# Prompt pages inside the first pair's compression products, head norms from two float32r parts, and the gates' two weight parts side by side

## The chip, the core and the metric

The kernel runs on one core of a Trainium2 chip. The metric is the device time of one execution in microseconds (us). Five engines work side by side, each through its own queue in order: PE (matrix products; PEld loads its weights), DVE (vector), ACT (scalar), POOL (GpSimd) and SP, which here only issues transfers. PE writes its products to banks of PSUM; DVE or ACT must read a bank out ("evacuate" it) before PE may reuse it.

## The reference, cut to what matters

Two layers of a decoder, for a prompt of 256 tokens and for 8 samples of 8 new tokens each, 320 columns together. The change lies in the input projection of layer 0 alone, whose parts are:

```python
z = jnp.einsum('btd,de->bte', h, W['w_in'])
rx, rg, q, kc, vc, ks, vs, kw, vw, gl = _split_even(z)
q  = _rmsnorm(q.reshape(b_, t, N_HEADS, HEAD_DIM), W['q_norm'])      # per head of 64
ks = _rmsnorm(ks.reshape(b_, t, N_KV, HEAD_DIM), W['k_norm'][1])     # kw likewise
gates = jax.nn.sigmoid(gl.astype(F32))                               # 48 columns

def _compress(k, pe, w1, w2):   # k: blocks of 64 tokens; the samples' come from cache pages
    kb = k.reshape(b_, t // BLOCK, BLOCK, N_KV, HEAD_DIM) + pe
    hid = jax.nn.gelu(jnp.einsum('bnjgd,jde->bnge', kb, w1))
    return jnp.einsum('bnge,ef->bngf', hid, w2)
```

`_compress` is done for keys and for values, over 64 cache pages of 128 tokens (of the samples) and the prompt's two pages of 128 tokens.

## The kernel before

**Products in three.** A float32 product is made from float32r parts: weights are split into `whi` (ACT, line 145) and `wlo` (DVE, line 146), activations into `yh` and `yl`, and PE does whi by yl, wlo by yh and whi by yh (lines 204 to 206). One such product has 128 by 128 weights and 320 columns.

**Groups and slots.** The projection goes in groups of 256 output columns, in the order kc, vc, ks, kw, q0, q1, q2, q3, gates (128 columns wide, though 48 are used), vs, vw. A group takes 16 steps of 128 rows of weights, 96 products. After every 24 of them (four steps) comes a **slot**: `side()` runs what the table `at(n, function, ...)` has put there, in the order in which the table was written. A group is four slots, the gates two; `E` holds each group's first slot after its last product: ks 12, kw 16, q0 20, q1 24, q2 28, q3 32, gates 34, vs 38. The work done in slots is in the program order of each engine, so it stands in the engine's queue between two stretches of 24 products.

**Evacuation.** At a group's end DVE multiplies its two banks by `rt` into SBUF (line 817 for k and v, line 882 for q). PE has three banks for groups, two in use by each, so the second half of the next group's first products needs the first of these two evacuations.

**Compression.** Cache pages come in four pairs (`bp` 0 to 3), each for keys and values (`i` 0, 1) in two halves of 8 pages (tile `cx`). `cmp_swap` rearranges a half into `cy` with four copies (line 703), two on DVE, one on POOL, one on ACT; `cmp_mm` multiplies it by `w1` (line 713: 16 steps by 2 outputs, 32 plain float32 products of 128 columns, of which the trace shows 64 rows, two each). The halves are swapped at the slot of a group's end and the next (12 and 13, 16 and 17, ...), the product comes two slots later (15, 19, ..., and 11 for the first). `cmp_mm` then adds the two outputs at once: a copy by ACT (line 719), an addition by DVE (line 720), twice. The prompt's pages and the position rows `pe` are a fifth pair with its own copies and its own products of 24 columns (slots 13 and 15). `w1` is loaded by SP (`cmp_load_w`, slots 7 and 11).

**Head norms.** For each 128 rows of k or q (two per group, "even" and "odd" below): ACT squares them (line 826, `hsq`, both in the slot of the group's end), PE sums over heads with a plain float32 product by the block matrix `blk1` (line 831), ACT takes the root (line 833), DVE the reciprocal (line 834) and the scaling (lines 845 and 847 for k, 891 and 895 for q). For q the even product is in the slot after the group's end and the odd one in the second; for k both are in the slot after.

Of the kernel before, what the change touches and what calls it, by code (L numbers as in the profile page):

```python
# [70 lines left out]
def tile_hybrid_step(ctx: ExitStack, tc: tile.TileContext, A, O, stop=None, dbg=None):  # L71
# [31 lines left out]
    plan(w_in, 0, 16, [4528], 128, 8)  # L103
# [33 lines left out]
    def w_conv():  # L137
        u, hf = divmod(st["conv"], 2)
        if st["dma"] == u:
            w_dma()  # L140
        st["conv"] += 1
        r = (raws.popleft() if hf else raws[0])[:, hf * HW:hf * HW + HW]
        h = wp.tile([128, HW], F32R, name="whi", bufs=NSP)
        l = wp.tile([128, HW], F32R, name="wlo", bufs=NSP)
        S.copy(h, r)  # L145
        (G if u < 4 and hf == 0 else V).tensor_tensor(l, r, h.bitcast(F32), ALU.subtract)  # L146
        convs.append((h, l))
# [65 lines left out]

    def run(gen):
# [10 lines left out]
    blk1 = cm[:, C_BLK:C_BLK + 128]  # L225
    ones = cst.tile([128, 128], F32, name="ones")
# [247 lines left out]
    rec = wab = None  # L474
# [3 lines left out]
    pct = cst.tile([128, 192], F32, name="pct")  # L478
# [3 lines left out]
    def rec_open():  # L482
        nonlocal rec, wab
        rec = rgp.enter_context(pool("rec"))
        wab = rec.tile([128, 2, 8, 128], F32, name="wab")
        SP.dma_start(wab[:, 0], A["rg_wa"][0].rearrange("h i j -> i h j"))
# [179 lines left out]
    def cmp_w():  # L666
# [3 lines left out]
        w2 = cmp_.tile([128, 128], F32, name="w2")  # L670
# [16 lines left out]
    def cmp_load_p():  # L687

        for i in range(2):
            cx[4, i, 0] = x = tok["kv"[i] + "c"]  # L690
            G.memset(x[64:128, 2], 0.0)
            SP.dma_start(x[0:64, 2], A["cmp_pe_" + "kv"[i]][0].rearrange("j g d -> j (g d)"))

    def cmp_swap(bp, i, hf, pages):
        v = cx.pop((bp, i, hf))[:, :pages].rearrange("p n (g s d) -> p (n g) s d", g=4, s=2)
        if bp == 4:
            cx["y", bp, i] = yf[:, 1560 * i:1560 * i + 768].rearrange("p (d h s n) -> p d h s n", h=1, s=2, n=12)
        elif hf == 0:
            cx["y", bp, i] = cmp_.tile([128, 32, 2, 2, 32], F32, name="cy")
        y = cx["y", bp, i][:, :, hf]  # L700
# [5 lines left out]
    def cmp_mm(bp, i, pages):  # L706

        y = cx.pop(("y", bp, i)).rearrange("p d h s n -> p d (h s n)")
        p = bank("a")
        n = pages * 8  # L710
# [4 lines left out]
        nh = min(pages, 8)  # L715
        for k in range(pages // nh):
            h = hid[64 * i:64 * i + 64, 16 * bp + 8 * k:16 * bp + 8 * k + nh].rearrange("p n g s -> p s (n g)")
            q = p[:, 64 * k:64 * k + 8 * nh].rearrange("p (s n) -> p s n", s=2)
# [3 lines left out]
    def cmp_gelu():  # L722
# [10 lines left out]
        cx["sq"] = cmp_.tile([128, 264], F32, name="csq")  # L733
        cx["vr"] = cmp_.tile([128, 4, 4, 4], F32, name="vr")
# [89 lines left out]
    def head_square(key, src):  # L824
        sq = evp.tile([128, N], F32, name="hsq", bufs=2)
        S.activation(sq, src, AF.Square)
        evt["sq", key] = sq

    def head_scale(key):
        p = bank("a")  # L830
        PE.matmul(p[:, :N], blk1, evt.pop(("sq", key)), start=True, stop=True)
        rs = evp.tile([128, N], F32, name="hrs", bufs=2)
# [4 lines left out]
    def k_square(b):  # L837
        for c in range(2):
            head_square((b, c), evt["k" + b][:, c])

    def k_norm(b):
        nm_ = "k" + b
        for c in range(2):
# [848 lines left out]
```

## Time and profile before

| | |
|---|---|
| time, median of 3 executions (lowest to highest) | 2909.09 us (2905.2 to 2910.19) |
| the profiled execution: its time, and its span from first to last instruction | 2911.25 us, 2909.6 us |
| PE busy, share of the span | 2846.3 us, 98% |
| DVE, ACT, POOL busy | 1618.6, 1213.1, 378.2 us |
| mean granted TensorE clock | 0.990 of full speed |
| moved by the DMA engines | 463.98 MB |

PE is busy nearly always, so a time is read as PE's products plus the waits between them. Rows of products overlap: a product's row lasts about 0.31 us while the next one starts 0.147 us later, so counts of starts tell the pace and not the rows' length.

### The profile page before, as it was taken

The page shows a single profiled execution, that of the slowest core. Times are in us where ns is not written, and L with a number is a line of the kernel's source. Part 1 is how long each engine was busy: PE and PEld are TensorE (multiplying, and loading weights), DVE is VectorE, ACT ScalarE, POOL GpSimd, SP SyncE. Part 2 cuts the span into 40 slices and gives each one's busy share as a digit, 9 for nine tenths or more (in the row PEclk, how much of TensorE's full clock was granted, in tenths as well). Part 3 has the DMA queues.
Part 4 walks back from the last instruction along what each step waited for, and adds up shares of the span by engine and source line. Part 5 has one row for each costly group of instructions (what it writes and reads, how often), then busy time and mean ns, then how long its engine had stood idle before and what let it go on. Part 6 is the DMA issues. An engine that isn't in the chain of part 4 may idle for free.

```text
span 2909.6 us, 53661 instructions
## 1 busy us (share of the span) xinstructions
PE 2846.3 (98%) x20947; PEld 2785.6 (96%) x20947; DVE 1618.6 (56%) x2937; ACT 1213.1 (42%) x2336; POOL 378.2 (13%) x555
## 2 busy tenths in 40 slices
PE   8999987999999999999999999999999999999999
PEld 7998776899999999999999999999999999999999
DVE  6796677774444544544465555555444444544544
ACT  4555644354334434434443333344433433433433
POOL 2323353230010010010010111111011011001000
PEclk9999989999999999999999999999999999999999
DMA  8765258645445555555445444444444444544543
GB/s 244 213 198 156 73 147 257 210 138 162 165 154 167 165 159 161 165 166 153 153 144 156 152 147 150 147 153 148 149 152 145 153 152 149 149 152 148 149 157 119
DMA packets 275997, 463.98 MB, mean 159 GB/s; under 512 B 19050, under 2 KB 100694, under 8 KB 275215
## 3 DMA queue, kind: packets, MB, share of 16 engines
q1 hardware_dynamic: 268254, 438.47, 49.1%
q0 software_dynamic: 6864, 19.44, 2.1%
q8 instruction: 164, 2.69, 0.4%
q10 hardware_dynamic: 624, 2.64, 0.2%
q14 instruction: 91, 0.74, 0.1%
HBM read 452.95 MB, written 15.92 MB: 161 GB/s over the span
## 4 chain that ended last, share of the span: by engine, by line
PE 81%; DVE 0%; DMA 0%; ACT 0%; issue 0%; DVEq 0%; ACTq 0%
PE ps_g L204 27%; PE ps_g L206 27%; PE ps_g L205 27%; DMA wraw<-in_w_out_e_dram 0%; PE ps_a L1652 0%; DVE wlo L146 0%; PE ps_a L1264 0%; PE ps_o L1325 0%; PE ps_a L1307 0%; DVE ktl L1168 0%; PE ps_a L633 0%; PE ps_a L1624 0%; DVE rs L1473 0%; PE ps_a L436 0%; DVE y L1475 0%
## 5 line engine op out<-in xcount | busy, mean ns | idle before, releaser
L146 DVE TENSOR_TENSOR wlo<-wraw,whi 128x512 fp32r<-128x512 f32 x1488 | 1007.4, 718 | 1122.3 <-ACT whi L145 1121.5
L145 ACT CAST whi<-wraw 128x512 fp32r<-128x512 f32 x1492 | 854.1, 617 | 1377.8 <-PE ps_g L206 1334.0
L204 PE MATMUL ps_g<-yl,whi 128*128 128x320 f32 x3408 | 1066.9, 313 | 10.9 <-DVE kv L817 5.1
L205 PE MATMUL ps_g<-yh,wlo 128*128 128x320 f32 x3408 | 1056.8, 310 | 0.0
L206 PE MATMUL ps_g<-yh,whi 128*128 128x320 f32 x3408 | 1056.6, 310 | 0.0
L204 PE MATMUL ps_g<-xl,whi 128*128 128x320 f32 x2560 | 796.2, 311 | 11.3 <-DVE xl L446 7.3
L206 PE MATMUL ps_g<-xh,whi 128*128 128x320 f32 x2560 | 792.7, 310 | 0.0
L205 PE MATMUL ps_g<-xh,wlo 128*128 128x320 f32 x2560 | 792.7, 310 | 0.0
L204 PEld LDWEIGHTS ps_g<-yl,whi 128*128 128x128 f32 x3408 | 643.2, 189 | 22.3 <-issue 8.4
L205 PEld LDWEIGHTS ps_g<-yh,wlo 128*128 128x128 f32 x3408 | 643.3, 189 | 1.7 <-issue 0.2
L206 PEld LDWEIGHTS ps_g<-yh,whi 128*128 128x128 f32 x3408 | 643.2, 189 | 0.0
L204 PEld LDWEIGHTS ps_g<-xl,whi 128*128 128x128 f32 x2560 | 482.4, 188 | 13.1 <-DVE xl L446 7.7
L205 PEld LDWEIGHTS ps_g<-xh,wlo 128*128 128x128 f32 x2560 | 482.4, 188 | 0.0
L206 PEld LDWEIGHTS ps_g<-xh,whi 128*128 128x128 f32 x2560 | 482.1, 188 | 0.0
L1477 POOL TENSOR_TENSOR y<-y,rs 128x320 f32<-128x320 f32 x96 | 92.3, 994 | 1257.8 <-DVE rs L1473 1257.8
L1473 DVE TENSOR_TENSOR rs<-ps_g,r 128x320 f32<-128x320 f32 x128 | 60.6, 488 | 25.1 <-PE ps_g L206 25.0
L1506 DVE TENSOR_TENSOR fr<-fr 128x320 f32<-128x320 f32 x128 | 62.3, 487 | 11.1 <-ACT xh L1509 11.1
L431 POOL TENSOR_TENSOR nacc<-nacc,nsq 128x320 f32<-128x320 f32 x45 | 44.1, 980 | 172.0 <-ACT nsq L427 170.4
L1507 DVE TENSOR_TENSOR xl<-fr,xh 128x320 fp32r<-128x320 f32 x128 | 62.9, 492 | 4.4
L1509 ACT ACTIVATE xh<-fr 128x320 fp32r<-128x320 f32 x128 | 60.3, 471 | 4.1
L1503 ACT ACTIVATE fr<-ps_g 128x320 f32<-128x320 f32 x128 | 56.1, 438 | 5.7 <-PE ps_g L206 5.7
L1586 POOL TENSOR_TENSOR xx<-cg,r 128x256 f32<-128x256 f32 x16 | 13.1, 819 | 278.4 <-DVE xx L1584 278.4
(382 smaller groups left out, 1426.3 us busy)
## 6 DMA issues: line engine op xcount, KB each, us to landing
wraw<-in_w_ff_dram SPq DMA_DIRECT2D x512, 512.0 KB, 3.7
wraw<-in_w_in_o_dram SPq DMA_DIRECT2D x96, 512.0 KB, 3.7
wraw<-in_w_in_e_dram SPq DMA_DIRECT2D x74, 512.0 KB, 5.3
wraw<-in_w_out_e_dram SPq DMA_DIRECT2D x32, 512.0 KB, 5.5
wraw<-in_w_out_o_dram SPq DMA_DIRECT2D x32, 512.0 KB, 3.9
cx<-in_cache_cmp_k_dram SPq DMA_DIRECT2D x64, 128.0 KB, 2.1
cx<-in_cache_cmp_v_dram SPq DMA_DIRECT2D x64, 128.0 KB, 3.4
kl<-in_cache_sel_k_dram SPq DMA_DIRECT2D x64, 128.0 KB, 3.6
```

The costliest lines, as they stand in the source:

```text
L145: S.copy(h, r)
L146: (G if u < 4 and hf == 0 else V).tensor_tensor(l, r, h.bitcast(F32), ALU.subtract)
L204: PE.matmul(ps[m][:, :N], wh, al, start=k + j == 0, stop=False)
L205: PE.matmul(ps[m][:, :N], wl, ah, start=False, stop=False)
L206: PE.matmul(ps[m][:, :N], wh, ah, start=False, stop=k + j == nk - 1)
L431: G.tensor_tensor(nacc["t"], nacc["t"], sq, ALU.add)
L1473: V.tensor_tensor(t, ps[:, :N], scale, ALU.mult)
L1477: after(1, lambda: G.tensor_tensor(y[:, c], y[:, c], t, ALU.add))
L1503: S.activation(t, ps[:, :N], AF.Relu)
L1506: V.tensor_tensor(t, t, t, ALU.mult)
L1507: V.tensor_tensor(xl[:, c], t, xh[:, c].bitcast(F32), ALU.subtract)
L1509: after(1, lambda: S.activation(xh[:, c], t, AF.Square))
```

## The change

Four things are changed, all in the input projection:

- The prompt's pages and the `pe` rows become columns 128 to 147 of the first pair's products (`cmp_swap_p`); the fifth pair and its products are gone. `pe` is no longer loaded into the token tile but into free space of `yf`, and it, `w1` and `w2` are loaded from POOL's queue and no longer from SP's.
- The additions behind a compression product (`cmp_evac`) are moved one slot later and joined into one copy and one addition for 128 columns; the first pair has two more small ones of each, for the prompt and `pe`.
- A head's squares are split into `hsh` (ACT) and `hsl` (DVE), and PE sums them in two float32r products by `blkr`, a copy of `blk1`. Only the even squares are made at the group's end; the odd ones are made in the slot after, behind the even reciprocal. For k the odd product moves to the second slot, as it was for q.
- The gates are planned as 64 columns. `whi` and `wlo` lie side by side as one set of 128 weights, so that two products (by yl and by yh) do what three did; `gate_evac` adds the two halves of the result.

```diff
-    plan(w_in, 0, 16, [4528], 128, 8)
+    plan(w_in, 0, 16, [4592], 64, 16)
...
+        if units[u][4] == 64:
+
+            for d, q in ((h, r[:, :256]), (l, r[:, 256:])):
+                d, q = (x.rearrange("p (k f) -> p k f", k=4) for x in (d, q))
+                S.copy(d[:, :, :64], q)
+                V.tensor_tensor(d[:, :, 64:], q, d[:, :, :64].bitcast(F32), ALU.subtract)
+            return
...
+    def gemm_64(act, evac):
+
+        ps = bank("g")
+        for hf in range(2):
+            w_fill()
+            st["half"] += 1
+            for i, w in enumerate(convs.popleft()):
+                for j in range(4):
+                    k = 8 * hf + 4 * i + j
+                    for m, x in enumerate(act(k)[::-1]):
+                        PE.matmul(ps[:, :N], w[:, 128 * j:128 * j + 128], x, start=k + m == 0, stop=k + m == 16)
...
-            SP.dma_start(w1[64 * hf:64 * hf + 64, i], A["cmp_w1_" + nm_][0][:, 32 * hf:32 * hf + 32])
-        SP.dma_start(w2[64 * i:64 * i + 64, 64 * i:64 * i + 64], A["cmp_w2_" + nm_][0])
+            G.dma_start(w1[64 * hf:64 * hf + 64, i], A["cmp_w1_" + nm_][0][:, 32 * hf:32 * hf + 32])
+        G.dma_start(w2[64 * i:64 * i + 64, 64 * i:64 * i + 64], A["cmp_w2_" + nm_][0])
...
+    def cmp_swap_p(i):
+
+        v = tok["kv"[i] + "c"][:, 0:2].rearrange("p n (g s d) -> p (n g) s d", g=4, s=2)
+        e = cx["pe"][:, i].rearrange("p (g s d) -> p g s d", g=4, s=2)
+        y = cx["y", 0, i]
+        for half in range(2):
+            h_ = slice(64 * half, 64 * half + 64)
+            for s_ in range(2):
+                (S.copy if s_ == half else V.tensor_copy)(
+                    y[h_, :, 128 + 8 * s_:136 + 8 * s_], v[64 * s_:64 * s_ + 64, :, half].rearrange("p n d -> p d n"))
+            G.tensor_copy(y[h_, :, 144:148], e[:, :, half].rearrange("p g d -> p d g"))
...
+        n = 128 if bp else 148
         for d in range(16):
             for u in range(2):
-                PE.matmul(p[64 * u:64 * u + 64, :n], w1[:, i, 16 * u + d], y[:, 16 * u + d],
+                PE.matmul(p[64 * u:64 * u + 64, :n], w1[:, i, 16 * u + d], y[:, 16 * u + d, :n],
                           start=d == 0, stop=d == 15)
...
+        if (bp, i) == (3, 1):
+            cmp_evac(bp, i, p)
+        else:
+            at(st["slot"] + 1, cmp_evac, bp, i, p)
...
     def head_square(key, src):
-        sq = evp.tile([128, N], F32, name="hsq", bufs=2)
+        sq = evp.tile([128, N], F32, name="hsq")
+        h = evp.tile([128, N], F32R, name="hsh", tag="hrs", bufs=2)
+        l = evp.tile([128, N], F32R, name="hsl")
         S.activation(sq, src, AF.Square)
-        evt["sq", key] = sq
+        split(h, l, sq)
+        evt["sq", key] = (l, h)
 
     def head_scale(key):
         p = bank("a")
-        PE.matmul(p[:, :N], blk1, evt.pop(("sq", key)), start=True, stop=True)
+        for i, x in enumerate(evt.pop(("sq", key))):
+            PE.matmul(p[:, :N], blkr, x, start=i == 0, stop=i == 1)
...
     def q_square(g):
-        for c in (2 * g, 2 * g + 1):
-            head_square(("q", c), evt["q", c])
+        head_square(("q", 2 * g), evt["q", 2 * g])
 
     def q_norm(c):
         t = evt["q", c]
         rs = head_scale(("q", c))
+        if c % 2 == 0:
+            head_square(("q", c + 1), evt["q", c + 1])
...
-            at(n + 6, cmp_mm, bp, i, 16)
+            at(n + 6, cmp_mm, bp, i)
...
-    at(E["vc"] + 2, cmp_load_p)
-    for i in range(2):
-        at(E["vc"] + 4, cmp_swap, 4, i, 0, 3)
-        at(E["vc"] + (7 if i else 5), cmp_mm, 4, i, 3)
+    at(CN + 1, cmp_load_p)
     for b in "sw":
         n = E["k" + b]
-        at(n, k_square, b)
-        at(n + 1, k_norm, b)
+        for c in range(2):
+            at(n + c, k_square, b, c)
+            at(n + 1 + c, k_norm, b, c)
```

DVE's queue over group q0, from its evacuation (line 882 before, 927 after) on; before:

```order
L882 TENSOR_TENSOR qr<-ps_g,rt 128x320 x2
L703 COPY cy<-cx 64x32x32 x2
L146 TENSOR_TENSOR wlo<-wraw,whi 128x512 x2
L703 COPY cy<-cx 64x32x32 x2
L834 RECIPROCAL hrs<-hrs 128x320
L891 SCALAR_TENSOR_TENSOR qp<-qr,qg,hrs 128x2x128
L895 SCALAR_TENSOR_TENSOR qbd<-qr,qg,hrs 64x8x8 x2
L146 TENSOR_TENSOR wlo<-wraw,whi 128x512 x2
L834 RECIPROCAL hrs<-hrs 128x320
```

and of the change:

```order
L927 TENSOR_TENSOR qr<-ps_g,rt 128x320 x2
L724 COPY cy<-cx 64x32x32 x2
L471 TENSOR_TENSOR hsl<-hsq,hsh 128x320
L762 TENSOR_TENSOR yr<-ps_a,yr 64x2x2x32
L154 TENSOR_TENSOR wlo<-wraw,whi 128x512 x2
L724 COPY cy<-cx 64x32x32 x2
L880 RECIPROCAL hrs<-hrs 128x320
L471 TENSOR_TENSOR hsl<-hsq,hsh 128x320
L937 SCALAR_TENSOR_TENSOR qp<-qr,qg,hrs 128x2x128
L941 SCALAR_TENSOR_TENSOR qbd<-qr,qg,hrs 64x8x8 x2
L154 TENSOR_TENSOR wlo<-wraw,whi 128x512 x2
L880 RECIPROCAL hrs<-hrs 128x320
```

The even low part `hsl` now stands behind the first two page copies, the odd one behind both pairs of copies, two weight splits and the even reciprocal; the joined addition (line 762) has come in front of the weight splits.

PE's queue in slot 13, which is behind the group ks (`ps_g` are the projection's banks, `ps_a` those of the work in slots; lines 211 to 213 of the change are 204 to 206 of before); before:

```order
L206 MATMUL ps_g<-yh,whi 128x320
L713 MATMUL ps_a<-yr,w_571 64x24 x32
L831 MATMUL ps_a<-hsq,cm 128x320 x2
L204 MATMUL ps_g<-yl,whi 128x320
L205 MATMUL ps_g<-yh,wlo 128x320
```

and of the change:

```order
L213 MATMUL ps_g<-yh,whi 128x320
L877 MATMUL ps_a<-hsl,blkr 128x320
L877 MATMUL ps_a<-hsh,blkr 128x320
L211 MATMUL ps_g<-yl,whi 128x320
L212 MATMUL ps_g<-yh,wlo 128x320
```

The prompt's 32 products of 24 columns are gone, the even norm's one product has become two, with the low part `hsl` first, and the odd norm's pair follows 24 products of the projection later.

POOL's queue from the output of kc on (slot 6); before:

```order
L862 DMA out_dram<-tok 128x2x256
L866 DMA out_dram<-tok 64x256
L703 COPY cy<-cx 64x32x32 x2
L862 DMA out_dram<-tok 128x2x256
L866 DMA out_dram<-tok 64x256
```

and of the change:

```order
L907 DMA out_dram<-tok 128x2x256
L911 DMA out_dram<-tok 64x256
L715 DMA yr<-in_cmp_pe_k_dram 64x256
L715 DMA yr<-in_cmp_pe_v_dram 64x256
L704 DMA w_571<-in_cmp_w_k_dram 64x2048 x2
L705 DMA yr<-in_cmp_w_k_dram 64x64
L724 COPY cy<-cx 64x32x32 x2
```

The loads of `pe` and of the keys' `w1` stand between the output of kc and POOL's first page copies.

## Rows read from the trace of the kernel before

**Rows 1.** The page, busy us of PE, its share of the span, its products.
```profile
PE 2846.3 (98%) x20947; PEld 2785.6 (96%) x20947; DVE 1618.6 (56%) x2937; ACT 1213.1 (42%) x2336; POOL 378.2 (13%) x555
```

**Rows 2.** PE's waits, 0 to 300 us: waiter, releaser, us, times, longest.
```profile
PE ps_g L204 <- DVE kv L817: 5.1, 2, 4.2
PE ps_a L713 <- DMA w<-in_cmp_w_k_dram: 4.1, 1, 4.1
...
PE ps_a L713 <- DVE yr L703: 2.5, 1, 2.5
```

**Rows 3.** Busy time by engine (starts), clock, DMA: between starts of compression products.
```profile
71.76:101.31 29.55, 27.03 (x228) 25.46 (x228) 21.45 (x27) 13.31 (x20) 8.63 (x8) 0.79 0.84 223
101.31:123.94 22.63, 21.72 (x236) 20.91 (x235) 15.94 (x19) 11.85 (x19) 6.56 (x6) 1.00 0.67 203
123.94:143.54 19.60, 19.60 (x172) 18.92 (x171) 17.95 (x22) 11.65 (x18) 8.89 (x7) 1.00 0.69 205
143.54:167.26 23.72, 20.80 (x166) 19.75 (x165) 22.66 (x29) 10.71 (x16) 4.06 (x2) 0.93 0.73 218
167.26:187.62 20.36, 19.25 (x165) 18.31 (x164) 19.17 (x25) 10.87 (x16) 4.48 (x2) 1.00 0.67 190
187.62:206.61 18.99, 18.99 (x165) 18.31 (x164) 17.97 (x23) 10.60 (x14) 4.17 (x2) 1.00 0.67 197
206.61:231.53 24.92, 20.69 (x170) 19.96 (x169) 19.27 (x29) 12.21 (x17) 4.08 (x2) 0.93 0.63 189
```

**Rows 4.** PE in order of time: start, us, product, count (rows overlap).
```profile
101.31 3.71 PE L713 MATMUL ps_a<-cy,w 128*64 128x128 f32 x64
104.86 2.00 PE L713 MATMUL ps_a<-yr,w 128*64 128x24 f32 x64
...
135.34 0.70 PE L831 MATMUL ps_a<-hsq,cm 128*128 128x320 f32 x2
139.40 0.70 PE L831 MATMUL ps_a<-hsq,cm 128*128 128x320 f32 x2
```

**Rows 5.** Busy time by engine, a stretch of projection products alone, 200 us.
```profile
1000.00:1200.00 200.00, 200.00 (x1365) 200.00 (x1365) 95.06 (x154) 75.15 (x138) 15.38 (x16) 1.00 0.53 163
```

**Rows 6.** DVE in order of time, from group q2's evacuation.
```profile
176.94 2.20 DVE L703 COPY cy<-cx 64x1024 f32<-64x1024 f32 x2
179.18 1.29 DVE L146 TENSOR_TENSOR wlo<-wraw,whi 128x512 fp32r<-128x512 f32 x2
180.39 2.20 DVE L703 COPY cy<-cx 64x1024 f32<-64x1024 f32 x2
182.62 2.15 DVE L834 RECIPROCAL hrs<-hrs 128x320 f32<-128x320 f32 x1
```

**Rows 7.** DVE groups by line and shape: count, busy us, mean ns.
```profile
L1507 DVE TENSOR_TENSOR xl<-fr,xh 128x320 fp32r<-128x320 f32 x128 | 62.9, 492 | 4.4
...
L720 DVE TENSOR_TENSOR yr<-ps_a,yr 64x64 f32<-64x64 f32 x16 | 3.5, 222 | 14.4 <-ACT yr L719 14.3
...
L845 DVE SCALAR_TENSOR_TENSOR kt_s<-kv,pbr,hrs 128x320 f32<-128x320 f32 x2 | 1.1, 552 | 0.1
```

**Rows 8.** DVE in order of time, page copies behind the evacuations of q0 and q3.
```profile
132.43 4.96 DVE L703 COPY cy<-cx 64x1024 f32<-64x1024 f32 x2
...
195.61 3.96 DVE L703 COPY cy<-cx 64x1024 f32<-64x1024 f32 x2
```

**Rows 9.** POOL in order of time, two of its page copies.
```profile
51.79 2.04 POOL L703 COPY cy<-cx 64x1024 f32<-64x1024 f32 x1 [0.36 <-issue]
...
196.53 2.11 POOL L703 COPY cy<-cx 64x1024 f32<-64x1024 f32 x1 [2.90 <-DMA cx<-in_cache_cmp_k_dram]
```

**Rows 10.** Busy time by engine, 3.4 us behind q1's evacuation wait.
```profile
155.90:159.30 3.40, 3.40 (x14) 3.24 (x13) 3.36 (x4) 3.37 (x4) 0.25 (x1) 0.50 0.78 257
```

**Rows 11.** SP's queue in order of time: issue of the keys' `w1`.
```profile
60.19 1.16 SPq L679 DMA_DIRECT2D w<-in_cmp_w_k_dram  x2
```

**Rows 12.** DMA issues by tile: count, KB each, median us to landing.
```profile
vl<-in_cache_win_v_dram POOLq DMA_DIRECT2D x8, 512.0 KB, 6.8
```

More of the change, by code (lines that the diff above doesn't have):

```diff
@@ L212, in gemm @@
                 yield
+    def gemm_64(act, evac):
[8 more added lines that the diff above has]
+                        PE.matmul(ps[:, :N], w[:, 128 * j:128 * j + 128], x, start=k + m == 0, stop=k + m == 16)
+            if hf:
+                evac(0, 0, ps)
+            step()
+            side()
+            yield
     def run(gen):
@@ L704, in cmp_swap, with cmp_mm, cmp_evac @@
                 y[64 * half:64 * half + 64, :, s_], v[64 * s_:64 * s_ + 64, :, half].rearrange("p n d -> p d n"))
-    def cmp_mm(bp, i, pages):
-        y = cx.pop(("y", bp, i)).rearrange("p d h s n -> p d (h s n)")
+    def cmp_swap_p(i):
[8 more added lines that the diff above has]
+            G.tensor_copy(y[h_, :, 144:148], e[:, :, half].rearrange("p g d -> p d g"))
+    def cmp_mm(bp, i):
+        y = cx.pop(("y", bp, i))
         p = bank("a")
-        n = pages * 8
+        n = 128 if bp else 148
         for d in range(16):
             for u in range(2):
-                PE.matmul(p[64 * u:64 * u + 64, :n], w1[:, i, 16 * u + d], y[:, 16 * u + d],
+                PE.matmul(p[64 * u:64 * u + 64, :n], w1[:, i, 16 * u + d], y[:, 16 * u + d, :n],
                           start=d == 0, stop=d == 15)
[L715 to L718, printed above, removed]
+        if (bp, i) == (3, 1):
+            cmp_evac(bp, i, p)
+        else:
+            at(st["slot"] + 1, cmp_evac, bp, i, p)
+    def cmp_evac(bp, i, p):
+        hi = hid[64 * i:64 * i + 64]
+        parts = [(hi[:, 16 * bp:16 * bp + 16].rearrange("p (k n) g s -> p k s (n g)", k=2),
+                  p[:, 0:128].rearrange("p (k s n) -> p k s n", k=2, s=2))]
+        if bp == 0:
+            parts += [(hi[:, 64:66].rearrange("p n g s -> p s (n g)"), p[:, 128:144].rearrange("p (s n) -> p s n", s=2)),
+                      (hi[:, 66, :, 0], p[:, 144:148])]
+        for h, q in parts:
             S.copy(h, q[64 - 64 * i:128 - 64 * i])
@@ L835, in head_scale, with k_square, k_norm @@
         return rs
[L837 to L841, printed above, removed]
+    def k_square(b, c):
+        head_square((b, c), evt["k" + b][:, c])
+    def k_norm(b, c):
         nm_ = "k" + b
-        for c in range(2):
+        if True:
             rs = head_scale((b, c))
@@ L901, in gate_evac @@
         t = evp.tile([128, N], F32, name="gt", tag="kv", bufs=3)
-        V.tensor_tensor(mirror(t[64:128]), halves(ps[64:128]), halves(rt[64:128]), ALU.mult)
-        V.tensor_tensor(t[64:128, NP_TOK:], ps[64:128, NP_TOK:N], rt[64:128, NP_TOK:], ALU.mult)
+        u = evp.tile([128, N], F32, name="gu", tag="hsl")
+        S.copy(u[64:128], ps[0:64, :N])
+        V.tensor_tensor(u[64:128], ps[64:128, :N], u[64:128], ALU.add)
+        V.tensor_tensor(mirror(t[64:128]), halves(u[64:128]), halves(rt[64:128]), ALU.mult)
+        V.tensor_tensor(t[64:128, NP_TOK:], u[64:128, NP_TOK:], rt[64:128, NP_TOK:], ALU.mult)
         S.activation(t[64:128], t[64:128], AF.Sigmoid)
@@ L923, in pre_q @@
         V.tensor_scalar(qg, par_k(0), 0.125, None, op0=ALU.mult)
+        S.copy(blkr, blk1)
         G.memset(qbd, 0.0)
```

44 lines of the change are left out of this document (22 added, 22 removed).

## The prediction

> **What bounds the kernel now.** I read the page's first part first: PE is busy 2846.3 us of the span of 2909.6, 98% [rows 1]. Only two things can move the time: the length of what PE does, and the some 60 us in which it waits or runs at half clock. A stretch with projection products alone gives their pace: 1365 in 200 us, 146.5 ns each [rows 5]. A slot (24 products) is then 3.52 us.
>
> The change touches only the stretch from the keys' `w1` to the last compression product but one, 60 to 232 us. In PE's waits there the reader should see two kinds: weights or columns that come late for a compression product (4.1 us on `w1`'s transfer, 2.5 on the prompt's copies) and evacuations that come late for the next group (5.1 in two waits on line 817, the longest 4.2) [rows 2]. Then I cut this stretch at the starts of the compression products [rows 3] and compared span, PE's busy time and clock of each piece. In 143.54 to 167.26 PE idles 23.72 − 20.80 = 2.9 us and the mean clock is 0.93; in 206.61 to 231.53 it idles 4.2 and the clock is 0.93; in 101.31 to 123.94 and 167.26 to 187.62 it idles 0.9 and 1.1 and the clock stays 1.00. So the longer waits were each followed by a time at the lower level (1.2 instead of 2.4 GHz), the short ones not. One such time lasts 3.40 us at 0.50 [rows 10] and so costs about 1.7 us more than the wait itself.
>
> DVE is the engine that PE waits for here, and its work in a stage of q is the second thing to see: two page copies 2.20, two weight splits 1.29, two more page copies 2.20, the even reciprocal 2.15, one behind the other from 176.94 to 184.77 [rows 6], and the odd reciprocal after that. That is when it is alone. The first pair of copies takes 4.96 behind q0 and 3.96 behind q3 [rows 8]; one of POOL's own copies runs at the time of the second of these, at 196.53 for 2.11 [rows 9].
>
> **Part 1, `w1` on POOL's queue.** SP issues it at 60.19 [rows 11], and PE waits until 71.76 [rows 2, 3]. On POOL's queue it is behind the output of kc and ahead of POOL's page copy, which begins at 51.79 in the trace [rows 9]; so it is issued about 8 us sooner. POOL's other transfers of 512 KB land in 6.8 us [rows 12], which puts it near 60, ahead of need: PE is ready at 71.76 − 4.1 = 67.7. The copies of the halves and of the prompt's columns are next in line, and end near 67 by the same rows. Gain **4.0 us**, and the first product then starts at 67.8. If the prompt's copies (short pieces on DVE, ACT and POOL ahead of this product) end late, this gain shrinks.
>
> The Trainium skill, "SBUF — State Buffer", section "SBUF: two separate sides", says that DVE's two-port modes on float32 copies hold a port shared with GpSimd, and that transfers whose descriptors GpSimd writes can stall behind them. By that, `w1` would still be late; it is rival C below. Here POOL's transfers of 512 KB land in 6.8 us with DVE busy, so the trace shows no such stall of that length.
>
> **Part 2, prompt as columns.** Two products of 24 columns go: 64 rows from 104.86 on, 2.00 us each [rows 4]. The two products of 148 columns get longer: 128 columns take (104.86 − 101.31)/64 = 55.4 ns a row [rows 4], 320 columns 146.5; in between, 148 columns come to 64.9 ns, 4.1 us instead of 3.55. Gone too is the wait of 2.5 for the prompt's copies and the half clock behind it; the mean clock of that stage was 0.79 [rows 3].
>
> **Part 3, head norms.** The old product is 4.06 us ahead of the next, 139.40 − 135.34 [rows 4], of which 3.52 are the 24 projection products: 0.54. Two float32r products cost 0.29. Twelve times this is 3 us of PE's work. But PE takes its instructions in order, and now must wait for `hsl`, which DVE makes. The even one stands behind the first pair of page copies, about in time when they take 2.20. The odd one is the matter. From the group's end: second evacuation about 0.6 (an estimate: 0.49 for one vector operation of this size [rows 7] and its start), then rows 6 from 176.94 to 184.77, 7.83, then what is new in the queue: even `hsl` 0.49, joined addition 0.3 (0.22 for half of its columns [rows 7]), odd `hsl` 0.49. Sum **9.7 us**. PE comes there after two slots and a pair, 3.52 + 0.29 + 3.52 = 7.33. It waits 2.4, where the old product needed only ACT's square and the trace shows no wait. Behind the waiting product stand all following projection products and the compression product.
>
> For ks, DVE has two copies of the prompt's or `pe`'s values (0.72 together, an estimate from the 0.22 and 0.49 of rows 7), the scaling of 0.55 [rows 7] with a short piece of 0.2, and 0.36 of the small additions besides: 11.55, wait 4.2. For kw 10.83, wait 3.5. For q3 one weight split less, 9.07; PE's two slots there are gates slots.
>
> **Part 4, gates.** 32 products for 48: 16 × 146.5 ns = 2.35 us less on PE. PE only comes sooner to the odd product of q3, where it waits 9.07 − 4.99 = 4.1 (4.99 = 2 × 2.35 + 0.29), so this saving is swallowed by the wait.
>
> **Part 5, later evacuations.** The joined addition moves behind the next slot's `hsl`; its result is read only behind the last compression product. It stands ahead of two weight splits and costs them 0.3; included above.
>
> **The sum.** A stage is the compression product, 3.52 to the group's end, the chain to the odd `hsl`, 0.29 and 3.52 to the next; the products for the output of ks and kw, 0.6, come in two (19.60 − 18.99 of two pieces of [rows 3] in which PE is busy throughout and that differ in them):
> ks 4.1 + 3.52 + 11.55 + 3.81 = 22.98 (29.55 before);
> kw 4.1 + 0.6 + 3.52 + 10.83 + 3.81 = 22.9 (22.63);
> q0 3.65 (3.55 with the step to the next work) + 0.6 + 3.52 + 9.72 + 3.81 = 21.3 (19.60);
> q1 and q2 20.7 each (23.72 and 20.36);
> q3 with 9.07 20.05 (18.99);
> vs 20.69 − 1.7 = 19.0, that is PE's busy time at full clock (24.92: there DVE had been behind by 4.2, and it catches up while PE waits for `hsl`).
> That is 147.7 for 159.8, with the earlier start **−16.1 us**.
> Two terms the rows bound without fixing them. The first copy pair takes 2.20, 3.96 or 4.96 [rows 6, 8]; the chains above have 2.20. The mean excess of the three is 1.5; POOL's copies have no reason to move out of the way, so I take it: six chains, **+9.0**; ends 0 and 16.6. And the clock: waits of 2.5 and more were followed by half clock, of 1.1 and less not. Six waits of 2.4 to 4.2 stand here; I take three at 1.7, **+5.1** (with some of the excess spent at the even product the wait is in two parts); ends 3.4 and 10.2.
> Sum: −16.1 + 9.0 + 5.1 = −2.0. The profiled execution took 2911.25, so 2909.2; the median is 2.2 under it: **2907 us**. The low end of all is −16.1 + 0 + 3.4 = −12.7, or 2896; the high end −16.1 + 16.6 + 10.2 = +10.7, or 2920.
>
> **Rivals.**
> A, the copies are undisturbed: PE's waits change when pages are loaded and POOL's copies fall into other times. Excess 0 to 0.5 for a chain, two or three drops of the clock: −16.1 + 1.5 + 4.3 = −10.3, **2899**. For it: 2.20 twice in rows 6. Against it: rows 8, and that all engines begin their copies at the same group end.
> B, each of the six waits costs the lower clock, and each chain about 1.7 of excess: −16.1 + 10.2 + 10.2 = +4.3, and with 2.3 of excess +7.9; **2915**, slower. It decides when the excess passes 1.9 in the mean with all six drops: −16.1 + 11.4 + 10.2 is +5.5, near 0.2% (5.8 us). For it: every wait here is 2.4 or more once any excess is added. Against it: the ones in rows 6.
> C, `w1` still late for the reason above: with the wait of 4.1 and the time at half clock behind it, 4.1 + 1.7 more than forecast: +3.8, **2913**. Against it: rows 12.
> D, PE never waits for the low parts, as DVE runs ahead: the six waits (4.2, 3.5, three of 2.4 and 4.1, in sum 19.0), the excess and the drops all go: −16.1 − 19.0 = −35, **2874**. Against it: DVE alone has 16 to 22.7 us of work in stages of 19 to 25 [rows 3].
> That the change doesn't do what it says is excluded for the removed products: they are not in PE's order.
>
> **How the numbers follow.** Forecast 0.45, A 0.28, B 0.16, C 0.07, D 0.04. Within 0.2% (5.8 us), about what a measurement of this kernel can tell from no change: three quarters of the forecast, some of A and C and a third of B. Faster: A mostly, D and a part of the forecast, 0.34; same 0.46; slower 0.20. The forecast's own range is 2901 to 2913; the range of 8 in 10 reaches to A's and B's: 2896 to 2918.
>
> **What would show it.** Right: the first product starts near 67.8 with no wait; PE waits on DVE's `hsl` at each odd product of the six stages, 2.4 to 4.2 us and more; no wait on evacuations behind q1 and vs; stages of 20 to 23 us; lower clock behind some of the odd products. Wrong: if the reciprocal or the copies come earlier in time than the group's end allows (DVE ahead), the waits are gone and D is near; if `w1` lands after 67.7, C; if the first pair of copies takes 2.2 in all stages, A.

## The result, and the profile after

The change made the kernel slower: 2925.07 us in the median of five executions (2923.07 to 2927.81) against 2909.09 before (five, 2905.2 to 2911.67), a ratio of 1.0056 with an interval of 1.0044 to 1.0068. The forecast was 2907, its range ended at 2918. The profiled execution of the change has a span of 2922.3 us; that of before had 2909.6.

PE's line on the page after, which answers to [rows 1]:

```profile
PE 2841.3 (97%) x20803; PEld 2779.6 (95%) x20803; DVE 1615.9 (55%) x2944; ACT 1218.2 (42%) x2346; POOL 381.5 (13%) x563
```

PE has 144 products and 5 us less of busy time than before, and the span is 12.7 us longer: 17.7 more of waiting.

PE's waits after, 0 to 300 us (us in total, times, longest), which answer to [rows 2]:

```profile
PE ps_a L877 <- DVE hsl L471: 23.9, 10, 7.7
PE ps_g L211 <- DVE kv L859: 3.3, 2, 2.7
...
PE ps_g L211 <- DVE qr L927: 2.2, 3, 0.8
PE ps_a L746 <- DVE cy L735: 1.0, 1, 1.0
```

The waits on `w1` and on the prompt's own products are gone, those on evacuations shorter; in their place PE stands 23.9 us at the norm products, for the low part `hsl`. The six waits at odd products are 7.7 (ks), 4.5 (kw), 2.0, 2.2, 1.9 (q0 to q2) and 1.1 (q3); four at even ones are 4.5 in sum, of which 2.2 in q3.

The stretches between the compression products after, which answer to [rows 3] (us, then busy us of PE, PEld, DVE, ACT, POOL, the granted clock, DMA):

```profile
70.76:99.56 28.80, 21.07 (x165) 20.40 (x165) 22.39 (x31) 14.22 (x24) 9.59 (x13) 0.88 0.88 250
99.56:129.00 29.44, 23.22 (x172) 22.03 (x171) 20.92 (x26) 12.76 (x21) 7.93 (x8) 0.88 0.58 175
129.00:154.16 25.16, 21.44 (x171) 20.28 (x170) 18.65 (x24) 12.27 (x19) 6.79 (x5) 0.93 0.43 127
154.16:177.98 23.82, 20.83 (x165) 19.68 (x164) 18.98 (x25) 11.70 (x17) 4.01 (x2) 0.93 0.75 230
177.98:201.68 23.70, 20.80 (x165) 19.67 (x164) 19.07 (x28) 11.78 (x19) 4.02 (x2) 0.93 0.48 129
201.68:223.20 21.52, 18.20 (x149) 17.34 (x149) 15.68 (x23) 11.71 (x16) 4.01 (x2) 0.92 0.73 225
223.20:245.00 21.80, 19.13 (x169) 18.44 (x168) 19.10 (x24) 11.39 (x15) 3.99 (x2) 1.00 0.39 110
```

Together 174.24 us for the 159.77 of before and the 147.7 of the forecast. The clock is below 1.00 in six of seven stages, where it was in three of them before. The last product of the stretch starts at 245.00 instead of 231.53, and what follows it takes 2677.3 instead of 2678.1: the loss lies wholly here.

How PE comes to wait in q1, on DVE in order of time, which answers to [rows 6]:

```profile
160.52 2.13 DVE L154 TENSOR_TENSOR wlo<-wraw,whi 128x512 fp32r<-128x512 f32 x1 [4.56 <-ACT whi L153]
162.57 0.88 DVE L927 TENSOR_TENSOR qr<-ps_g,rt 128x320 f32<-128x320 f32 x2
163.37 2.19 DVE L724 COPY cy<-cx 64x1024 f32<-64x1024 f32 x2
165.60 0.49 DVE L471 TENSOR_TENSOR hsl<-hsq,hsh 128x320 fp32r<-128x320 f32 x1
166.12 0.29 DVE L762 TENSOR_TENSOR yr<-ps_a,yr 64x128 f32<-64x128 f32 x1
166.45 1.29 DVE L154 TENSOR_TENSOR wlo<-wraw,whi 128x512 fp32r<-128x512 f32 x2
167.66 2.20 DVE L724 COPY cy<-cx 64x1024 f32<-64x1024 f32 x2
169.89 2.15 DVE L880 RECIPROCAL hrs<-hrs 128x320 f32<-128x320 f32 x1
171.96 0.43 DVE L471 TENSOR_TENSOR hsl<-hsq,hsh 128x320 fp32r<-128x320 f32 x1
```

From the end of the evacuation, 163.45, to the odd low part, 172.39, it takes 8.94 us. PE's last product of q1 had ended at 161.59, so the evacuation itself came late, behind the weight split in the first line, and from the group's end it is 10.8 us. That line shows the other half of the matter too: DVE had been idle for 4.56 us behind ACT, and ACT for PE, which still held a weight buffer. Of all waits of the change, 0 to 300 us:

```profile
ACT whi L153 <- PE ps_g L213: 55.9, 27, 5.0
DVE wlo L154 <- ACT whi L153: 44.3, 25, 6.4
```

In the trace of before the same two are 17.9 and 23.6 us. PE waits for DVE, and then DVE for PE; the time that PE stands is not time in which DVE gets ahead.

### The profile page after: what moved, and what is told of

Its sections match the earlier page's. It is cut to its first block, busy times and chain, and to the rows that moved or that the text cites. A ratio compares the mean times of both kernels' runs of the same rounds, so it can differ in the third digit from the quotient of the medians.

```text
span 2922.3 us, 53382 instructions
## 1 busy us (share of the span) xinstructions
PE 2841.3 (97%) x20803; PEld 2779.6 (95%) x20803; DVE 1615.9 (55%) x2944; ACT 1218.2 (42%) x2346; POOL 381.5 (13%) x563
## 4 chain that ended last, share of the span: by engine, by line
PE 86%; DVE 6%; ACT 2%; issue 2%; DMA 2%; SPq 1%; POOL 0%; DVEq 0%; ACTq 0%; POOLq 0%
PE ps_g L211 28%; PE ps_g L212 28%; PE ps_g L213 28%; DVE wlo L154 2%; DVE cy L724 1%; DMA wraw<-in_w_in_e_dram 1%; PE ps_a L746 1%; PE ps_a L1314 1%; SPq L710 0%; ACT whi L153 0%; DVE hrs L880 0%; ACT ps L1141 0%; SPq L685 0%; PE ps_o L1375 0%; ACT ps L1139 0%
```

## The experiments

Medians of all, with the kernel before as it ran beside each. In the last column is the start of the last compression product of the stretch in the one profiled execution; what follows that product, the same work in all, took 2676.3 to 2682.0 us (2687.7 in lo_unread), so a single profile tells a difference of some us at best. Kernels with different numbers in the column "before" ran in different groups; between those the ratios are the safer comparison.

| kernel | median us (executions) | before | ratio, interval | last product |
|---|---|---|---|---|
| the change | 2925.07 (5) | 2909.09 | 1.0056, 1.0044 to 1.0068 | 245.00 |
| norm_only | 2925.22 (4) | 2906.73 | 1.0060, 1.0043 to 1.0077 | 242.48 |
| norm_old | 2905.36 (10) | 2906.73 | 0.9989, 0.9980 to 0.9999 | 218.92 |
| odd_late | 2921.17 (4) | 2906.73 | 1.0049, 1.0032 to 1.0066 | 238.19 |
| squares_first | 2909.07 (10) | 2906.73 | 1.0005, 0.9996 to 1.0015 | 224.44 |
| odd_sooner | 2914.49 (10) | 2908.48 | 1.0023, 1.0013 to 1.0033 | 225.77 |
| after_act | 2942.86 (4) | 2908.48 | 1.0117, 1.0099 to 1.0135 | 259.00 |
| norm_old_act | 2899.79 (9) | 2908.48 | 0.9969, 0.9959 to 0.9980 | 219.41 |
| w1_pool | 2910.16 (10) | 2908.48 | 1.0008, 0.9998 to 1.0018 | 228.86 |
| gates_only | 2906.80 (11) | 2907.43 | 1.0004, 0.9995 to 1.0014 | 224.03 |
| no_gates | 2899.86 (7) | 2907.43 | 0.9974, 0.9963 to 0.9986 | 220.34 |
| evac_now | 2902.69 (11) | 2907.43 | 0.9986, 0.9977 to 0.9995 | 218.48 |
| squares_first_act | 2917.69 (6) | 2907.43 | 1.0038, 1.0024 to 1.0051 | 235.85 |
| lo_unread | 2914.56 (10) | 2907.95 | 1.0020, 1.0011 to 1.0030 | 227.62 |
| columns_only | 2901.51 (11) | 2907.95 | 0.9981, 0.9972 to 0.9990 | 222.30 |
| no_gates_act | 2897.93 (5) | 2907.95 | 0.9963, 0.9949 to 0.9976 | 221.64 |

### Is it the head norms? Undone, and alone

norm_old: the change with the norms' functions and places as they were before.

```diff
-        for i, x in enumerate(evt.pop(("sq", key))):
-            PE.matmul(p[:, :N], blkr, x, start=i == 0, stop=i == 1)
+        PE.matmul(p[:, :N], blk1, evt.pop(("sq", key)), start=True, stop=True)
...
-        head_square(("q", 2 * g), evt["q", 2 * g])
+        for c in (2 * g, 2 * g + 1):
+            head_square(("q", c), evt["q", c])
```

> The change with its third part undone: head norms by one plain float32 product from ACT's square, both squares at the group's end; the other parts as in the change. Theory 1 (PE's waits for the low parts, 23.9 us in ten, and the lower clock behind six of them, cost the time): these waits are gone, PE's products get 3 us longer, DVE has 12 subtractions of 0.49 us less; 2925 - 24 - 10 + 3 = 2894 us, if waits for evacuations take some of it back up to 2903. Theory 2 (DVE and POOL in each other's way are the bound; the waits only moved to where PE meets DVE first): waits on evacuations take the place of those on the low parts, and the time stays within 6 us of 2925. Theory 3 (the loads from POOL's queue or the columns of the prompt cost it): also within 6 us of 2925.

norm_only: the same edit the other way, on the kernel before.

> The kernel before with the third part alone: two float32r products by hi and lo squares, odd squares in the slot after. Theory 1: PE waits for the low part at each odd product, as in the change, with the lower clock behind it; 2909 + 15 to 30 = 2924 to 2939 us. Theory 2: DVE has 12 subtractions (6 us) more in about the same order and PE meets it elsewhere; 2909 to 2915. Theory 3: no change, 2909 within 4 us.

PE's longest wait of norm_only, 60 to 260 us:

```profile
PE ps_a L836 <- DVE hsl L447: 16.5, 11, 2.8
```

By the medians the norms alone cost 18.5 us, and taking them out of the change gives 19.7 back (19.5 by the ratios). So they are the whole loss, with or without the other parts. Theory 3 is out. Theory 1 had the sign and, for norm_only, the size; but norm_old was expected at 2894 to 2903 and took 2905, and in its trace, 60 to 260 us, waits on evacuations remain:

```profile
PE ps_g L211 <- DVE kv L858: 5.1, 2, 3.8
PE ps_g L211 <- DVE qr L923: 4.2, 3, 3.1
```

### Is it where the low part stands, or the work for it?

squares_first puts both squares and their four parts ahead of the page copies:

```diff
+    for b in "sw":
+        for c in range(2):
+            at(E["k" + b], k_square, b, c)
+    for g in range(4):
+        at(E[f"q{g}"], q_square, g)
...
-        sq = evp.tile([128, N], F32, name="hsq")
+        sq = yf[:, N * (key[1] % 2):N * (key[1] % 2) + N]
```

> The change with both squares and their two parts made at the group's end ahead of the page copies (in buffers that take the place of others). hi and lo parts stay. Theory 1 (not the two parts themselves but their place behind page copies and weight splits in DVE's queue costs the time): both low parts are ready some 2 us after the group's end, no wait at any norm product, page copies 1 us later; 2925 - 24 - 10 = 2891 us, up to 2900 if evacuations are waited for instead. Theory 2 (DVE is full in any order): 2918 to 2926, with waits of the same sum on evacuations.

PE's waits of squares_first, 60 to 260 us:

```profile
PE ps_g L211 <- DVE qr L927: 5.0, 2, 3.5
PE ps_a L959 <- ACT gt L952: 2.8, 1, 2.8
PE ps_a L845 <- DVE kt_s L890: 2.4, 1, 2.4
PE ps_a L845 <- DVE kt_w L890: 2.3, 1, 2.3
...
PE ps_a L877 <- DVE hsl L471: 1.4, 2, 1.0
```

The same work in another order: 23.9 us of waits for `hsl` become 1.4, and 14.8 of the 19.5 us come back by the ratios (16 by the medians). The amount of work is worth the other 4.7 at most. The expectation, 2891 to 2900, was missed all the same: PE's other waits are 16.1 us, of which the first four lines are 12.5, where they were 6.5 in the change. The edit also gives these tiles other buffers, so by itself it does not show that the order alone did it; the next one leaves the buffers as they were.

odd_sooner only exchanges two neighbours: the odd parts (`f` is the odd `head_square`) ahead of the even root and reciprocal.

```diff
         for i, x in enumerate(evt.pop(("sq", key))):
             PE.matmul(p[:, :N], blkr, x, start=i == 0, stop=i == 1)
+        if f:
+            f()
         rs = evp.tile([128, N], F32, name="hrs", tag="hrs", bufs=2)
```

> The change with two neighbours on DVE and on ACT exchanged: the odd square's parts are made ahead of the even norm's root and reciprocal instead of behind them. DVE's work and PE's order stay word for word the same otherwise. Theory 1 (how late the odd low part stands in DVE's queue sets the wait): the low part is ready 2.2 us sooner for q and 2.9 sooner for k, so the odd waits shrink from about 20 us in six to about 6 to 8, and those of q and q3 no longer draw the lower clock; 2925 - 13 - 5 = 2907 us, within 4. Theory 2 (DVE's amount of work is the bound): 2921 to 2926, the waits turn up on evacuations.

2914.5: 10.6 of the 18 expected (9.6 by the ratios). Its profiled execution was its fastest (2904.45), so it likely shows the waits at their shortest: 12.2 us for `hsl` in eight. The order alone, with buffers and work unchanged, is worth that much; theory 1's direction holds, its size was too large, and theory 2 is out.

lo_unread leaves the low part's product out, and DVE goes on making the part:

```diff
-        for i, x in enumerate(evt.pop(("sq", key))):
-            PE.matmul(p[:, :N], blkr, x, start=i == 0, stop=i == 1)
+        PE.matmul(p[:, :N], blkr, evt.pop(("sq", key))[1], start=True, stop=True)
```

> The change with the low part made as before by DVE but not read: a head's sum is one product by the high part, so the output lacks the low parts' share. DVE, ACT and their order are the same; PE waits only for ACT's high part, ready 2.2 us (q) to 2.8 us (k) before the low one in the trace of the change, and has 12 products (1.8 us) less. Theory 1 (PE's wait for the low part): 2925 - 14 - 2 - 4 of clock = 2905 us, within 4. Theory 2 (DVE's amount of work): 2921 to 2924.

PE's longest waits of lo_unread, 60 to 260 us:

```profile
PE ps_a L876 <- ACT hsh L470: 10.8, 4, 5.5
PE ps_g L211 <- DVE qr L926: 5.7, 3, 3.4
```

10.5 us come back with DVE's work unchanged, 1.8 of them for the 12 products that are gone (in the profile the stretch is 17.4 us shorter and what follows it 10.4 longer). It is half of the 20 expected. Of the rest, 10.8 us of waiting stay because the odd high part is late too: ACT squares the odd half behind its own copies and the even root. Waits on evacuations are 10.1 us, where they were 5.5 in the change. It is not DVE's subtraction alone; the odd square is started only in the slot after.

odd_late moves each odd product one slot later, behind the compression product.

```diff
-            at(n + 1 + c, k_norm, b, c)
-        at(n + 3, kv_out, "k" + b)
+            at(n + 1 + 2 * c, k_norm, b, c)
+        at(n + 4, kv_out, "k" + b)
...
-        at(n + 2, q_norm, 2 * g + 1)
+        at(n + 3, q_norm, 2 * g + 1)
```

> The change with every odd norm product one slot later, behind the compression product of that slot (and the outputs of ks and kw one slot later); everything else the same, DVE's order too but for the odd reciprocal and scaling. Theory 1 (what counts is how much projection work lies between the group's end and the odd product: 7.3 us in the change, the low part is ready after 10 to 15): now 7.3 + 3.5 + 3.65 = 14.5 us lie there, so the odd waits vanish but for ks, the even ones (5.5 us) stay; 2925 - 18 - 8 = 2899 us, within 5. Theory 2: the waits move to evacuations or weights, 2920 to 2926.

PE's waits of odd_late, 60 to 260 us:

```profile
PE ps_a L877 <- DVE hsl L471: 10.7, 3, 3.7
PE ps_g L211 <- DVE qr L927: 5.9, 3, 3.0
PE ps_a L960 <- ACT gt L953: 4.3, 1, 4.3
PE ps_a L746 <- DVE cy L735: 2.3, 1, 2.3
```

Only 4 us by the medians, 2 by the ratios, whose intervals overlap: no gain that can be told from nothing, and here theory 1 fell as it stood. The odd waits are gone, all three waits for `hsl` that are left are at even products. But DVE's reciprocal and scaling of the odd half now come late too, and its copies behind the next evacuation met POOL's. On DVE and POOL, in order of time, in odd_late:

```profile
128.47 5.49 DVE L724 COPY cy<-cx 64x1024 f32<-64x1024 f32 x2
```

```profile
127.14 2.35 POOL L724 COPY cy<-cx 64x1024 f32<-64x1024 f32 x1
...
131.15 1.92 POOL L724 COPY cy<-cx 64x1024 f32<-64x1024 f32 x1
```

Two copies took 5.49 us and not 2.2, the even low part behind them was late by that, and PE waited 3.4 us for it. Letting the consumer come later helped little here, where the producer's queue was then later as well; bringing the producer forward (squares_first, odd_sooner) helped.

### POOL's copies, taken away

The edit in all three is one word, on three bases: after_act is the change with it, norm_old_act and squares_first_act are norm_old and squares_first with it. The expectations stand in this order.

```diff
-            (V.tensor_copy, G.tensor_copy, V.tensor_copy, S.copy)[k](
+            (V.tensor_copy, S.copy, V.tensor_copy, S.copy)[k](
```

> The change with POOL's page copy of each half given to ACT, so that POOL copies nothing while DVE copies. Theory 1 with the excess as its second term (DVE stands still while POOL copies, some 1.5 to 3 us once or twice in a stage, and the low parts come later by that): chains to the odd low part get 1 to 1.5 us shorter in most stages, the clock falls still; 2925 - 7 - 3 = 2915 us, within 4. If POOL's copies take nothing from DVE: 2923 to 2928 (ACT has 2 us more in each stage).

> The version with the old norms (parts 1, 2, 4 and 5 of the change) and POOL's page copies on ACT. It took 2905 with them on POOL; waits for evacuations of 3.4 and 4.1 us were left in its trace, behind DVE operations that took 4 us instead of 1 while POOL copied. If POOL's copies are what eats the gain of the other parts: those waits go and the lower clock behind them, 2905 - 7 - 3 = 2895 us, within 4. If DVE's work alone is the bound: 2902 to 2907.

> The change with both squares and their parts made at the group's end ahead of the page copies, and POOL's page copies on ACT: the two experiments that gained, together. With both low parts ready before ACT's and DVE's copies, ACT's longer copies no longer stand ahead of a part that PE waits for (they did when they alone were moved, which cost 18 us). Theory 1: no wait at a norm product, few at evacuations, 2909 - 6 = 2903 us, within 4; against the old norms with the same copies (2900) it has 3 us less on PE and 6 more on DVE. If ACT's amount of work is what cost those 18 us: over 2915.

With the old norms this gained 5.8 us by the ratios (0.9989 to 0.9969, intervals that just touch), between the two expectations. With the new ones it cost 17.8, and my expectation of a gain was wrong: the chain to the low part ran over ACT, which I had not put on it. ACT, then DVE, in order of time, in the change with its copies on ACT:

```profile
142.47 0.46 ACT L470 CAST hsh<-hsq 128x320 fp32r<-128x320 f32 x1
```

```profile
139.37 2.17 DVE L724 COPY cy<-cx 64x1024 f32<-64x1024 f32 x2
142.96 0.49 DVE L471 TENSOR_TENSOR hsl<-hsq,hsh 128x320 fp32r<-128x320 f32 x1 [1.42 <-ACT hsh L470]
...
148.92 2.15 DVE L880 RECIPROCAL hrs<-hrs 128x320 f32<-128x320 f32 x1 [1.78 <-ACT hrs L879]
```

ACT's copies stand ahead of its square and ahead of its root, DVE idles 1.42 and 1.78 us for them, and the sum shows at the norm products: 36.5 us of waits for `hsl` instead of 23.9. It is the same mechanism with another engine as the late one, and a strong sign that a chain and not an amount sets this time: in the stretch ACT is busy 116 of 189 us here and 112 of 149 in norm_old_act, which has nearly the same work on ACT and is the faster by 43 us. In squares_first_act the norm products' waits are down to one of 2.6 us, but 2918 was far over the 2903 expected and inside the range that I had given to the rival, ACT's amount of work. DVE there idles behind ACT's root and, for the joined addition, behind ACT's copy (1.7 to 2.4 us a time), while ACT is busy 113.5 of 166 us. That speaks for its order and against its amount, but no run has the one without the other.

### The other parts, one by one

w1_pool: the loads of `w1` and `w2` by POOL, on the kernel before.

```diff
-            SP.dma_start(w1[64 * hf:64 * hf + 64, i], A["cmp_w1_" + nm_][0][:, 32 * hf:32 * hf + 32])
+            G.dma_start(w1[64 * hf:64 * hf + 64, i], A["cmp_w1_" + nm_][0][:, 32 * hf:32 * hf + 32])
```

> The kernel before with the loads of w1 and w2 issued by POOL instead of SP, and nothing else. The prediction's first part gives -4.1 us of wait and about 1.7 of lower clock behind it, unless the next in line (page copies ending near 67) takes a part: 2908 - 4 = 2904 us, within 3. If a transfer issued by POOL is late while DVE copies, or something else is waited for at the same place: 2908 within 2.

```profile
PE ps_g L204 <- DVE kv L817: 6.7, 3, 4.1
PE ps_a L713 <- DVE yr L703: 4.5, 1, 4.5
```

The wait of 4.1 for `w1` is gone from PE's waits (above, 60 to 260 us), and the median did not move beyond its interval: the prompt's copies are waited for 4.5 us instead of 2.5 and line 817 6.7 instead of 5.1. Nor was the 4.1 a fixed amount. With the load issued by SP as before, PE waits 2.1 us for `w1` in norm_only's trace, 1.0 in that of gates_only and not at all in that of columns_only, where it comes to this product only at 71.36.

columns_only: the prompt's columns on the kernel before, with `w1` on SP and the evacuations right behind their products. It is no_gates (below) with the edit of w1_pool turned round and that of evac_now.

> The second part alone on the kernel before: the prompt's pages as columns of the first pair, w1 still issued by SP, evacuations right behind their products, old norms and gates. If the columns are what gains in the other parts: 2900 to 2903 us. If the earlier w1 is needed for it too (it moved nothing alone, where the prompt's own products then waited longer): 2904 to 2908.

gates_only: the gates' part on the kernel before. no_gates: norm_old without it (`gate_evac` as before, too). The cut is that of no_gates:

```diff
-    plan(w_in, 0, 16, [4592], 64, 16)
+    plan(w_in, 0, 16, [4528], 128, 8)
...
-    run(gemm_64(yact, gate_evac))
+    run(gemm(1, 16, yact, gate_evac, 128))
```

> The kernel before with the fourth part alone: the gates' high and low weight parts side by side, 32 products for 48. PE has 2.35 us less in a stretch in which (in the trace of before) it does not wait. If nothing takes its place: 2908.5 - 2.4 = 2906 us. If DVE and ACT are behind there and PE only meets them sooner (evacuations, gate transposes behind the two more operations of the gates' evacuation): 2908 to 2911.

> The version with the old norms (parts 1, 2, 4, 5) without the gates' part: parts 1, 2 and 5 on the kernel before. It tells where the gain that the prediction gave them went: 10 us in its first stage, 4.1 at the start. If the prompt's columns gain what they should and nothing takes it back: 2897 to 2900 us. If their gain is taken by later waits on evacuations: 2905 to 2909, as with the gates (2905).

evac_now: norm_old with `cmp_evac` called at once.

```diff
-        if (bp, i) == (3, 1):
-            cmp_evac(bp, i, p)
-        else:
-            at(st["slot"] + 1, cmp_evac, bp, i, p)
+        cmp_evac(bp, i, p)
```

> The version with the old norms (parts 1, 2, 4, 5) without the later evacuations: the joined copy and addition of a compression product stand right behind it again, ahead of the weight splits of that slot. If the later place is worth something, it is DVE's idle time behind ACT's copy: 0.5 us in each of seven stages, 2905 + 3 = 2908 us. If it is hidden, 2905 within 2.

The columns carry the gain, 6.4 us, as expected. The gates' part alone is within the interval of nothing, and in norm_old it costs some 4 (0.9989 with it, 0.9974 without; the intervals overlap). The trace of gates_only from the compression product behind q2 on, against the last two of [rows 3], shows it given and mostly taken back:

```profile
180.95:197.59 16.64, 16.64 (x149) 15.96 (x148) 15.71 (x19) 9.83 (x13) 4.28 (x2) 1.00 0.69 210
197.59:224.03 26.44, 20.83 (x170) 19.80 (x169) 20.80 (x33) 12.23 (x17) 4.02 (x2) 0.94 0.58 168
```

2.35 us less in the stage of q3 (18.99 before), 1.5 more in the next (24.92). Whether it really costs 4 in norm_old is open: there the two stages are as long with it as without it (42.8 and 43.1 us), and the profiles differ in what follows. The later evacuations are worth nothing here: 0.9986 undone, 0.9989 with them.

no_gates_act: no_gates with the page copies on ACT, the edits that gained together.

> Parts 1, 2 and 5 on the kernel before (old norms, old gates) with POOL's page copies on ACT. Without the last step it took 2900 us, and with the gates' part and the last step also 2900. If the two gains (5 us each) lie at different places, 2895; if both took away the same waits on evacuations behind q1, gates and vs, 2900.

2897.9, the lowest median of all: 10.0 us under before and 27 under the change. Against no_gates it is about 3 better by the ratios, with overlapping intervals: the two gains do not add up to the 2895 that they would give at different places, and at the same place would be 2900; it lies between.

## Why the prediction was wrong, by its steps

- **PE waits for the odd low part at each of six stages**: right, and at every one. The chain was sized at 9.7 us for q and found at 9.5 behind an evacuation in time (0.6 and the 8.94 above). The ten waits are 23.9 us; the forecast's six were 19.0, and the excess on top of them 9.0. In the stages, length over the forecast's bare sum is 174.24 − 147.7 = 26.5; without the clock (13.6, next) and without the last stage (2.8), 10.1 are left for the excess of 9.0.
- **The excess, in the first pair of page copies**: about the right size, but by luck, since it lies elsewhere. Only two of the six pairs are clearly longer than 2.2:

```profile
109.95 3.15 DVE L724 COPY cy<-cx 64x1024 f32<-64x1024 f32 x2
...
138.96 3.05 DVE L724 COPY cy<-cx 64x1024 f32<-64x1024 f32 x2
```

  That is 1.8 us. In the other four stages they take 2.1 to 2.2, the sign that the prediction gave for rival A, and A did not come. What is longer is a weight split: in kw and in q0 to q3 the one ahead of the evacuation takes 2.1 to 2.2 instead of 0.69 us (160.52 above), and in ks one takes 2.56.
- **The clock, "I take three at 1.7, +5.1"**: this step failed. In the change:

```profile
90.90:97.70 6.80, 3.88 (x14) 3.89 (x15) 6.54 (x8) 2.17 (x5) 0.99 (x2) 0.50 0.49 151
121.60:128.40 6.80, 6.19 (x23) 6.19 (x24) 6.46 (x8) 1.65 (x3) 1.96 (x4) 0.50 0.64 203
148.90:152.30 3.40, 3.40 (x14) 3.40 (x14) 3.35 (x6) 1.03 (x2) 0.00 (x0) 0.50 0.18 62
```

  All six stages have one such time at 1.2 GHz, 27.2 us in sum, which is 13.6 at most for 5.1 (PE was busy in 23.7 of it, which makes 11.8; the excess is then larger by the difference). Rival B had just this, six falls; at 1.7 each it still came out short, since two lasted 6.8 us. The waits that I left out at 2.4 were enough: those of 1.9 to 2.2 in q0 to q3 were each followed by one. From two kinds of examples (2.5 and more, 1.1 and less) nothing could be told of the lengths between, and I chose the middle. No length settles it either. The wait of 2.7 on the evacuation of vs, in the change, was not followed by a fall up to 254 us, nor was one of 3.45 in odd_sooner (at 195.86, its stage at 1.00). Two stages of squares_first show it too, which hold the waits of 2.4 on line 890 for ks and of 2.3 for kw:

```profile
90.55:113.77 23.22, 20.12 (x171) 19.27 (x171) 20.64 (x26) 12.93 (x23) 8.13 (x8) 1.00 0.68 203
113.77:136.87 23.10, 20.79 (x172) 20.16 (x171) 19.82 (x25) 13.40 (x22) 8.68 (x9) 0.93 0.63 194
```

- **The last stage, 19.0**: it took 21.8. The wait on the evacuation of vs is still there, 2.7 instead of 4.2; DVE had not caught up while PE waited. It had waited for PE's weight buffers in turn (4.43 us in q3, as the 4.56 above), then 2.4 for ACT's root, and two small scalings of line 941 took 4.1 instead of 0.7 us beside POOL's copies. Which of these counts is not shown.
- **The start at 67.8**: it was 70.76. `w1` was in time, so rival C is out; the copies next in line were not, and [rows 9], from which I had them end near 67, shows none of the columns' copies. POOL's of the `pe` columns, in the change:

```profile
68.48 1.69 POOL L737 COPY cy<-yr 64x128 f32<-64x128 f32 x2
```

  They end at 70.17, and DVE's of the prompt, for which PE waits 1.0 us, at 70.40. The prediction had named this as the way in which the gain would shrink. The other 2 us are earlier in that one execution, where PE ran a stretch at half clock ahead of the first product (0.61 in the mean from 40 to 44 us).
- **Sum of what was mis-sized**: 13.6 − 5.1 = 8.5 of clock, 2.8 in the last stage, 3.0 at the start, 1.1 of excess: 15.4. The forecast for the profiled execution was −2.0, the stretch gave +13.5.
- **Gates "swallowed by the wait"**: right that nothing is left of it, but gates_only shows the same without that wait, so the reason is not confirmed. **Later evacuations at nothing**: right.
- **What the sum had no term for**, the waits next in line: the old norms with all other parts should by the forecast's own terms have gained 32 us (16.1 + 19.0, less 3 for the longer products), and gained 1.4 by the medians and 3.2 by the ratio. Its terms for the norms are then 30 (19.0 + 9.0 + 5.1 − 3), and the norms cost 19.5. Two sums that were both too large stood against each other, so the forecast came nearer than its parts. Rival D has the same gap: squares_first nearly removed the waits for `hsl`, and took 2909, not 2874. In norm_old's profile the stretch is 10.7 us shorter than before, where the forecast's sums without the six waits give 12.1 + 19.0, less 3 for the longer products; and the part behind it is 3.2 longer. DVE is next in line in most stages: in five of the seven there, of 19.6 to 26.2 us, it is busy 19.3 to 23.5. I had priced the removed waits as if the next one behind them were nothing.

What stays open: why the clock fell behind some of PE's waits of 1.9 to 3.5 us and not behind others; what makes the part behind the stretch differ by up to 10 us; and why one and the same kernel spreads over 10 to 17 us (norm_old, odd_sooner) where others keep to 5.

## What to carry to other kernels

When a product's operand moves from an engine that is idle to one with a full queue, walk that queue from the event that releases it and compare with PE's arrival; put small producers that PE waits for ahead of bulk copies, since here the same work in another order was worth about 15 us, and an exchange of two neighbours alone about 10. A wait of PE can cost more than its length, in clock and in the weight buffers that it holds back from the engine it is waiting for (no run prices the second). And a wait removed at the front is worth only its distance to the next one: 4.1 us for `w1` came to nothing measurable in w1_pool.

## What was not expected of the hardware

POOL's two page copies in q1, in the change:

```profile
158.10 4.01 POOL L724 COPY cy<-cx 64x1024 f32<-64x1024 f32 x2 [17.05 <-DMA cx<-in_cache_cmp_k_dram]
```

They end at 162.11. A weight split of DVE that takes 0.69 us alone started at 160.52 and took 2.13, to 162.65: it ended only 0.54 us after POOL's copy had. In odd_late two page copies took 5.49 instead of 2.2. The delay fell on splits, copies or small scalings, whichever were there, in q1 on the last one ahead of the evacuation that PE waits for. An evacuation, which reads PSUM, was not held: q0's took its usual 0.89 us from 138.16 on, while POOL copied from 135.54 to 140.00. The Trainium skill, "SBUF — State Buffer", section "SBUF: two separate sides", calls the pair of ports that DVE and GpSimd share an exclusive lock, for the whole of an instruction; the trace agrees (162.11 and 162.65 above). No run here shows the stall of transfers issued by POOL, which the same page tells of: `w1` was not waited for. Giving these copies to ACT gained 5.8 us with the old norms and lost 17.8 with the new.
